# A hybrid mLSTM, attention and expert layer: SBUF pools padded to multiples of 256 bytes

## The chip, the core and the metric

The kernel runs on one core of a Trainium2 chip. The metric is the time that the device needs for one execution, in microseconds (us). The engines have short names in the profile: PE is TensorE (matmuls), PEld its weight loads, DVE is VectorE, ACT is ScalarE, POOL is GpSimd, SP is SyncE, which here only issues transfers. SBUF is the memory that the engines work from: 128 partitions, and a tile has the same byte address in each of its partitions. PSUM is the memory into which PE writes.

## The reference

One encoder layer on 512 tokens of width 2048, in float32, cut here to what matters:

```python
proj = jnp.einsum("bsd,dc->bsc", x, w_in[i])            # 2048 -> 4640 columns
h_mlstm = _mlstm_mixer(mq, mk, mv, mo, mg, ...)         # 8 heads, both directions
h_attn = _axial_gqa(aq, ak, av, g_q[i], g_k[i])         # 8 query heads, 2 key heads of 128
x = _layer_norm(ALPHA * x + concat([h_mlstm, h_attn]) @ w_out[i], ...)
moe = _expert_choice_moe(x, w_router[i], w_gate[i], w_up[i], w_down[i])   # 16 experts, 64 tokens each
pl = sigmoid(x @ w_pl_gate[i] + b_pl_gate[i]) * (p[i] @ w_pl_proj[i])
x = _layer_norm(ALPHA * x + moe + pl, ...)
```

Each expert has three weight matrices of 8 MB (2048 x 1024 gate and up, 1024 x 2048 down); with the gate of pl they are about 400 MB, read once.

## The kernel before, in words

The kernel is written with tiles: a pool is a stretch of SBUF that is opened and closed like a stack, on the left or on the right side, and a tile is a piece of a pool with a name; `bufs` says how many buffers a name has. A scheduler orders the instructions of each engine by their due times and what they depend on, sets the waits, and places a tile in a buffer when the one before it has been read for the last time. Each engine works through its own list in order.

**The projections** (`gemm`, line 178; its matmul is line 197). Each weight block of 512 rows comes into a tile wraw (SP's queue), ACT copies it rounded to fp32r into wH (line 150, `split`) and DVE puts the rest into wL (line 151); the left operand x is split in the same way into xH and xL. Each product is made of three fp32r matmuls: high x high, high x low, low x high. The tiles wraw, wH and wL have two buffers each and take 8 KB of a partition. The attention projection (`attn_proj`, first to run) has four chunks of 392 columns, so a weight tile holds four rows of 392 values, 1568 bytes apart: 4 chunks x 4 blocks x 4 row tiles x 4 rows x 3 are 768 matmuls. The output gate, q and k, v and the two halves of w_out have 512 columns, 1920 matmuls.

**The attention** (`attention`, line 281). Rotary position and norm come group by group (`rope_group`, line 259): ACT squares each head (line 266) into a tile jk that nobody reads, summing into ss; POOL turns the sums into a scale (`pow_rstd`, line 147). First the two key heads (ssk, rk), then the query heads in three groups, (6, 7), (3, 4, 5), (0, 1, 2), each with its own tiles ssq and scq; after each group its heads (`attn_head`, line 314): scores, exp on ACT with scale scq (line 336), the product with v, and a store of oT to DRAM on POOL's queue (line 354). The scheduler lays all this beside the projection of the output gate (`o_proj`, line 356).

**The mLSTM** works from q and k after a convolution (line 478), its gates are turned with the matrix jrev (lines 394, 438, 443), and each head ends with squares into hjk (line 613). Then come w_out in two halves (`mix_attn`, `mix_mlstm`), the layer norm of x1 (`ln1_tile`, with the statistics st and the transposed factors lnT) and the router.

**The experts** (`phase_b`, line 1107) are most of the second half. Weights come as tiles of 1 MB, 8 KB in each of 128 partitions, through a ring of 13 places (`ring_tile`, line 657): four tiles r, opened on the right side for it, the six tiles rw, which are the places of wraw, wH and wL, then l1g, l1b and r3. SP's queue fills them in the order in which they are used: an expert takes 8 gate, 8 up and 8 down tiles (lines 928 and 950) and one of the gate of pl (line 848), and the small tile plp (line 851). PE works through them in a fixed order: gate and up (line 984), pl (line 898) mixed with the sum over the tokens of the expert before (line 1071), down (line 1035). The tokens of an expert are fetched from x1d by an indirect transfer of POOL (line 957).

**Where the tiles lie.** By the memory map of the program, every tile takes a multiple of 32 bytes. The left side begins with small constants; the pool of wraw, wH and wL begins at byte 17824, which is 69 x 256 + 160. All its six tiles lie 160 bytes past a multiple of 256, and so does the first tile of each pool that is set on it. The right side ends at byte 229344, 224 bytes past a multiple of 256: the tiles xH and xL, fa, r, l1g, l1b and r3 all lie at 224. In a weight tile of 392 columns the four rows lie at 160, 192, 224 and 0.

Of the kernel before, what the change touches and what calls it, by code (L numbers as in the profile page):

```python
# [11 lines left out]
F32 = mybir.dt.float32  # L12
# [8 lines left out]
S = 512  # L21
D = 2048
NT = 4
KT = 16
# [69 lines left out]
class Body:  # L94
# [25 lines left out]

    def dump(self, name, t):
        if name in self.dbg:
            self.nc.gpsimd.dma_start(self.dbg[name], t)

    def setup(self):
        nc, a = self.nc, self.a
        c = self.pool("consts")
        self.c = c
        self.ident = c.tile([128, 128], F32, name="ident")
        nc.gpsimd.dma_start(self.ident, a["ident"])  # L130
        self.jrev = c.tile([128, 128], F32, name="jrev")
        nc.gpsimd.dma_start(self.jrev, a["jrev"])
        self.hf = c.tile([128, 1], F32, name="hf")
        nc.gpsimd.dma_start(self.hf, a["half"])
        self.mhalf = c.tile([128, 64], F32, name="mhalf")
        nc.vector.memset(self.mhalf, -0.5)
        d = self.pool("dram", space=DRAM)
        self.ftd = d.tile([D, S], F32, name="ftd")
        self.od = d.tile([S, 1024], F32, name="od")
        self.md = d.tile([16, S], F32, name="md")  # L140
        self.part = d.tile([S, D], F32, name="part")
        self.x1d = d.tile([S, D], F32, name="x1d")
        self.ps = self.pool("psA", space=PSUM)
# [82 lines left out]
    def attn_proj(self):  # L226
        nc = self.nc
        self.mg = self.pool("mgate")
        self.pA = self.pool("projA")
        self.proj = self.pA.tile([128, NT, 1568], F32, name="proj")  # L230
        for ch in (3, 2, 1, 0):
            c0 = ch * 392

            def evac(i, p, c0=c0):
                nc.scalar.copy(self.proj[:, i, c0:c0 + 392], p)

            self.gemm(self.win(3072 + c0, 392), self.xH, self.xL, 392, evac,
                      first=ch == 3)
# [20 lines left out]
    def rope_group(self, nm, c0, n, ss):  # L259
        nc = self.nc  # L260
        ct, st = self.rope[nm]
        for i in range(NT):
            v = self.proj[:, i, c0:c0 + n * 128]
            for h in range(n):
                jk = self.at.tile([128, 128], F32, name="jk", bufs=2)
                nc.scalar.activation(jk, v[:, h * 128:(h + 1) * 128], AF.Square,
                                     accum_out=ss[:, i, h:h + 1])
            v3 = v.rearrange("p (n d) -> p n d", n=n)
            t1 = self.at.tile([128, n, 128], F32, name="t1", bufs=1)
            t2 = self.at.tile([128, n, 128], F32, name="t2", bufs=1)  # L270
            nc.vector.tensor_mul(t1, v3, ct[:, i][:, None, :].to_broadcast([128, n, 128]))
            v5 = v.rearrange("p (n a h f) -> p n a h f", n=n, a=2, h=2)
            t5 = t2.rearrange("p n (a h f) -> p n a h f", a=2, h=2)
            s4 = st[:, i].rearrange("p (a h f) -> p a h f", a=2, h=2)
            for h in range(2):
                nc.vector.tensor_mul(t5[:, :, :, h], v5[:, :, :, 1 - h],
                                     s4[:, :, h][:, None].to_broadcast([128, n, 2, 32]))
            nc.vector.tensor_add(v3, t1, t2)

    def attention(self):  # L280
        nc = self.nc
        self.attn_tables()
        self.at = self.pool("attn")
        at = self.at
        ssk = at.tile([128, NT, 2], F32, name="ssk")
        rk = at.tile([128, NT, 2], F32, name="rk")
        self.rope_group("g_k", GK, 2, ssk)
# [14 lines left out]
        for h0, n in ((6, 2), (3, 3), (0, 3)):  # L302
            ssq = at.tile([128, NT, n], F32, name=f"ssq{h0}")
            scq = at.tile([128, NT, n], F32, name=f"scq{h0}")
            self.rope_group("g_q", GQ + h0 * 128, n, ssq)
            nc.vector.tensor_scalar_add(ssq, ssq, 128 * EPS)
            self.pow_rstd(scq.rearrange("p a b -> p (a b)"), ssq.rearrange("p a b -> p (a b)"))
            for h in range(h0, h0 + n):
                self.attn_head(h, scq, h - h0, kH, kL, vH, vL)

    def attn_head(self, h, scq, hi, kH, kL, vH, vL):
        nc, at = self.nc, self.at
# [8 lines left out]
        for half in range(2):  # L321
            PTH = at.tile([128, NT, 256], F32R, name="PTH", bufs=2)
            PTL = at.tile([128, NT, 256], F32R, name="PTL", bufs=2)
            for q in range(2):
# [5 lines left out]
                nc.tensor.matmul(sp, qL[:, sl], kH[:, kv], start=False, stop=True)  # L330
                sm = at.tile([128, 4], F32, name="sm", bufs=4)
                nc.vector.reduce_max(sm[:, 0:1], sp, axis=AX.X)
# [44 lines left out]
    def gates(self):  # L377
        nc, a = self.nc, self.a
# [3 lines left out]
        g = self.pool("gwork", side="right")  # L382
        G = []
        for nm, b in (("i", "b_i"), ("f", "b_f")):
            t = self.G[nm]
            bt = g.tile([64, 1], F32, name="b" + nm)
            nc.vector.memset(bt, 0.0)
# [67 lines left out]
    def qk_proj(self):  # L455
        nc = self.nc
# [3 lines left out]
        self.QL = self.mq.tile([128, NH, S], F32R, name="QL")  # L460
        cw = self.mq.tile([128, 8, 5], F32, name="cw")
        nc.gpsimd.dma_start(cw, self.a["convT"])
        cv = self.pool("conv")
        lo, hi = slice(0, 64), slice(64, 128)
        for ch in range(2):
            def evac(i, p, ch=ch):
# [3 lines left out]

                r = cv.tile([128, S + 4], F32, name="cr", bufs=2)
                nc.gpsimd.memset(r[:, 0:2], 0.0)
# [108 lines left out]
    def mlstm_num(self, h, ml, hh, P, off, half):  # L581
        nc = self.nc
        pn = [self.ps.tile([128, 512], F32, name=nm, bufs=1) for nm in ("t", "o")]
        for dr in range(2):
            for q in range(2):
                tb = half * 2 + q
                sbs = list(range(0, tb + 1) if dr == 0 else range(tb, NT))
                for k, sb in enumerate(sbs):
                    b = off[dr][sb] + (tb - sb if dr == 0 else tb)
                    nc.tensor.matmul(pn[dr][:, q * 130:(q + 1) * 130],  # L590
                                     P[dr][:, b * 128:(b + 1) * 128], self.v1[:, sb, h],
                                     start=k == 0, stop=k == len(sbs) - 1)
        r = ml.tile([128, 2, 2], F32, name="hr", bufs=4)
        for dr in range(2):
# [12 lines left out]
    def mlstm_post(self, h, ml, hh, o):  # L607
        nc = self.nc
        ss = ml.tile([128, NT], F32, name="hss", bufs=2)
        rs = ml.tile([128, NT], F32, name="hrs", bufs=2)  # L610
        for tb in range(NT):
            jk = ml.tile([128, 128], F32, name="hjk", bufs=1)
# [9 lines left out]
        f = ml.tile([128, S], F32, name="mw", bufs=MW)  # L622
# [47 lines left out]
    def mix_mlstm(self):  # L670
        nc, a = self.nc, self.a
        accp = self.pool("acc")
        self.acc = accp.tile([128, NT, D], F32, name="acc")
        self.st = accp.tile([128, NT, 4, 6], F32, name="bst")
        self.x1T = accp.tile([128, KT, S], F32, name="x1T")
# [3 lines left out]
        nc.gpsimd.dma_start(self.wr[:, :, :NE], a["w_router"])  # L679
        self.lnT = accp.tile([128, 2, KT], F32, name="lnT")  # L680
        nc.gpsimd.dma_start(self.lnT, a["ln1T"])
        self.af = accp.tile([48, 256], F32, name="af")
# [3 lines left out]
        self.bpl = accp.tile([128, KT], F32, name="bpl")  # L686
        nc.gpsimd.dma_start(self.bpl, a["b_plT"])
        fm = self.pool("fm")
        self.close("pa", "fa", "mls2")
        self.r1 = self.pool("r1", side="right")  # L690
        lp = self.r2 = self.pool("r2", side="right")
        g = lp.tile([128, D], F32, name="l1g")
# [412 lines left out]
    def phase_b(self):  # L1105
# [5 lines left out]
        self.sq2 = wk.tile([128, NT, len(LASTW)], F32, name="sq2")  # L1111
        self.m0 = wk.tile([128, NT], F32, name="m0")
        self.r3 = self.pool("r3", side="right")
# [134 lines left out]
```

## Time and profile before

| | us |
|---|---|
| median of 3 runs | 1850.37 |
| lowest and highest of the 3 | 1849.45 and 1853.31 |
| the profiled execution, its own time | 1849.9 |
| its span, from the first to the last instruction | 1847.7 |

| engine | busy us, share of the span | instructions |
|---|---|---|
| PE | 1767.0 (96%) | 8208 |
| PEld | 1039.4 (56%) | 8208 |
| DVE | 755.7 (41%) | 1358 |
| ACT | 408.4 (22%) | 810 |
| POOL | 194.2 (11%) | 255 |

A matmul is counted as busy from its start to a modelled end, and matmuls overlap, so the pace of a row of matmuls is read from the distance of their starts. An fp32 matmul runs as two passes, an fp32r matmul as one, and the profile counts passes. DMA share is the mean busy share of the core's 16 transfer engines; sums of packets that just touch can give 1.01. [...]

### The profile page before, as it was taken

How to read it: one execution, taken by the hardware profiler on the slowest of the kernel's cores; microseconds unless marked ns; L12 is line 12 of the kernel's file. 1: busy time of each engine (PE TensorE's matmuls, PEld its weight loads, DVE VectorE, ACT ScalarE, POOL GpSimd, SP SyncE). 2: the span in 40 equal slices, each digit the busy share in tenths (PEclk: the TensorE clock that was granted, in tenths of full speed). 3: DMA queues.
4: the chain of work that ended last, by engine and by line, in shares of the span. 5: the costliest groups of instructions: out<-in, count | busy, mean ns of one | idle time of the engine just before them, and what ended most of it. 6: DMA issues, size and time to landing. Idle time of an engine off the chain costs nothing.

```text
span 1847.7 us, 20774 instructions
## 1 busy us (share of the span) xinstructions
PE 1767.0 (96%) x8208; PEld 1039.4 (56%) x8208; DVE 755.7 (41%) x1358; ACT 408.4 (22%) x810; POOL 194.2 (11%) x255
## 2 busy tenths in 40 slices
PE   8999999999999999899999999999999999999991
PEld 7998888877777887543443444344334434433441
DVE  4446563593466445711331333133223213322346
ACT  3435453343565212200000000000000000000013
POOL 2000101251133100510000000000000000000004
PEclk9999999999999999989999999999999999999996
DMA  6332223223554782589999999999999999999992
GB/s 219 111 95 95 80 84 94 81 92 98 167 166 133 233 347 92 212 332 409 420 420 420 420 420 420 419 420 420 419 420 420 419 420 421 420 420 419 420 376 91
DMA packets 114066, 535.03 MB, mean 290 GB/s; under 512 B 10641, under 2 KB 26050, under 8 KB 61490
## 3 DMA queue, kind: packets, MB, share of 16 engines
q1 hardware_dynamic: 106082, 504.14, 69.0%
q0 software_dynamic: 7024, 24.07, 3.5%
q10 hardware_dynamic: 864, 5.51, 0.7%
q8 instruction: 64, 1.05, 0.2%
q14 instruction: 32, 0.26, 0.0%
HBM read 514.77 MB, written 18.91 MB: 289 GB/s over the span
## 4 chain that ended last, share of the span: by engine, by line
PE 71%; DMA 19%; DVE 4%; POOL 2%; issue 2%; ACT 2%; SPq 0%; POOLq 0%; ACTq 0%; DVEq 0%
PE g L197 29%; PE pl L898 11%; DMA plp<-in_w_pp_dram 10%; PE py L1035 8%; PE pg L984 5%; DMA r<-in_w_up_dram 5%; PE pu L984 4%; PE pc L1071 3%; DMA rw<-in_w_up_dram 3%; PE plq L892 2%; PE o L350 1%; DMA l1g<-in_w_up_dram 1%; DMA l1b<-in_w_up_dram 1%; PE t L342 1%; ACT mw L540 1%
## 5 line engine op out<-in xcount | busy, mean ns | idle before, releaser
L1073 DVE TENSOR_TENSOR acc<-acc,pc 128x512 f32<-128x512 f32 x240 | 164.6, 687 | 123.9 <-PE pc L1071 122.2
L197 PE MATMUL g<-wH,xH 128*128 128x392 f32 (+1 forms) x512 | 191.2, 375 | 8.9 <-ACT wH L150 8.9
L197 PE MATMUL g<-wH,xL 128*128 128x392 f32 (+1 forms) x512 | 190.4, 372 | 0.0
L151 DVE TENSOR_TENSOR wL<-wraw,wH 128x1024 fp32r<-128x1024 f32 (+2 forms) x114 | 126.4, 1144 | 156.5 <-ACT wH L150 156.5
L197 PE MATMUL g<-wL,xH 128*128 128x392 f32 (+1 forms) x512 | 190.3, 372 | 0.1
L1071 PE MATMUL pc<-ys,oh 128*128 128x512 f32 x240 | 185.6, 774 | 1.1 <-DVE acc L1073 0.9
L150 ACT CAST wH<-wraw 128x1024 fp32r<-128x1024 f32 (+2 forms) x114 | 106.6, 976 | 217.3 <-PE g L197 206.0
L1056 DVE SCALAR_TENSOR_TENSOR ys<-py,gate,ys 64x512 fp32r<-64x512 f32 (+2 forms) x70 | 49.3, 704 | 195.8 <-ACT ys L1052 194.6
L898 PE MATMUL pl<-x1T,rw 128*128 128x512 f32 x224 | 112.3, 592 | 0.0
L197 PEld LDWEIGHTS g<-wH,xH 128*128 128x128 f32 x512 | 97.0, 190 | 19.8 <-ACT wH L150 9.9
L984 PE MATMUL pg<-rw,xeT 128*64 128x512 f32 x480 | 106.0, 593 | 0.0
L957 POOL DMA_INDIRECT xe<-x1d,idx x16 | 15.3, 954 | 857.1 <-PE pc L970 856.7
L1035 PE MATMUL py<-rw,hT 128*64 128x512 f32 x472 | 104.2, 594 | 0.0
L197 PEld LDWEIGHTS g<-wL,xH 128*128 128x128 f32 x512 | 97.1, 190 | 11.1 <-DVE wL L151 1.1
L197 PEld LDWEIGHTS g<-wH,xL 128*128 128x128 f32 x512 | 97.1, 190 | 10.4 <-issue 0.2
L1052 ACT ACTIVATE ys<-py,gate 64x512 fp32r<-64x512 f32 (+2 forms) x70 | 45.2, 646 | 247.2 <-PE py L1035 189.3
L898 PE MATMUL pl<-x1T,r 128*128 128x512 f32 x192 | 98.0, 592 | 0.0
L984 PE MATMUL pu<-rw,xeT 128*64 128x512 f32 x432 | 96.2, 593 | 0.9 <-DMA rw<-in_w_up_dram 0.9
L984 PE MATMUL pg<-r,xeT 128*64 128x512 f32 x416 | 93.3, 600 | 0.0
L990 DVE TENSOR_TENSOR hs<-hs,pu 128x512 f32<-128x512 f32 x16 | 11.0, 688 | 201.2 <-PE pu L984 201.2
L984 PE MATMUL pu<-r,xeT 128*64 128x512 f32 x416 | 92.3, 593 | 1.0 <-DMA r<-in_w_up_dram 1.0
L989 DVE TENSOR_TENSOR hs<-hs,pg 128x512 f32<-128x512 f32 x16 | 11.0, 688 | 176.3 <-ACT hs L988 176.3
(350 smaller groups left out, 2706.8 us busy)
## 6 DMA issues: line engine op xcount, KB each, us to landing
rw<-in_w_gate_dram SPq DMA_DIRECT2D x60, 1024.0 KB, 14.2
rw<-in_w_down_dram SPq DMA_DIRECT2D x59, 1024.0 KB, 17.7
rw<-in_w_up_dram SPq DMA_DIRECT2D x54, 1024.0 KB, 17.9
r<-in_w_gate_dram SPq DMA_DIRECT2D x52, 1024.0 KB, 19.5
r<-in_w_up_dram SPq DMA_DIRECT2D x51, 1024.0 KB, 17.4
r<-in_w_down_dram SPq DMA_DIRECT2D x41, 1024.0 KB, 17.7
wraw<-in_w_in_dram SPq DMA_DIRECT2D x24, 1024.0 KB, 5.0
wraw<-in_w_out_dram SPq DMA_DIRECT2D x16, 1024.0 KB, 7.0
```

The costliest lines, as they stand in the source:

```text
L150: self.nc.scalar.copy(H, src)
L151: self.nc.vector.tensor_sub(L, src, H.bitcast(F32))
L197: self.lastM = nc.tensor.matmul(ps[i][:, :m], l, r, start=beg and q == 0, stop=end and q == 2)
L342: nc.tensor.transpose(pt[:, kb * 128:(kb + 1) * 128], P[:, kb * 128:(kb + 1) * 128], self.ident)
L892: self.pe(nc.tensor.matmul(pp, wp[:, k], self.pT[:, k], start=k == 0, stop=k == 1))
L898: self.pe(nc.tensor.matmul(pg, W[:, k], self.x1T[:, k], start=k == 0, stop=k == KT - 1))
L984: self.pe(nc.tensor.matmul(p[f * 64:(f + 1) * 64], x, lst[g][:, j * 1024 + f * 512:j * 1024 + (f + 1) * 512], start=g == 0 and j == 0, sto ...
L1035: self.pe(nc.tensor.matmul(py[c][n * 64:(n + 1) * 64], hT[:, q // 4, q % 4], Dn[q][:, n * 1024 + c * 512:n * 1024 + (c + 1) * 512], start= ...
L1052: self.lastW = nc.scalar.activation(ys[n][own], py[own], AF.Copy, scale=self.gate[own, e:e + 1])
L1056: nc.vector.scalar_tensor_tensor(ys[n][oth], py[own], self.gate[own, e:e + 1], ys[n][own].bitcast(F32), op0=ALU.mult, op1=ALU.subtract)
L1071: self.pe(nc.tensor.matmul(pc, oh[:, i * 128:(i + 1) * 128], y, start=True, stop=True))
L1073: nc.vector.tensor_add(d, d, pc)
```

## The change

The change alters where tiles lie. A tile of 24 values and one of 56 values are put in as padding, on the left side and on the right; small tiles are made wider (`small` takes a wider tile and hands out its first n columns), the tile cr gets 64 spare columns instead of 4, and a last padding tile closes the first part of the pool acc. After it the ring, the weight tiles, x's halves, the pools' first tiles and nearly all the rest lie on multiples of 256 bytes; the rows of a weight tile of 392 columns lie at 0, 32, 64 and 96. To make room, jk has one buffer instead of two, and the three pairs ssq and scq, which had a name for each group, become two buffers of one name. jrev moves from the constants into the pool mgate (its load is then written after load_x), and the statistics st and lnT to the end of acc's first part. The function `dump`, which nothing calls, goes.

```diff
--- before.py
+++ after.py
@@ -118,9 +118,9 @@
         for n in reversed(list(self.open)):
             self.close(n)
 
-    def dump(self, name, t):
-        if name in self.dbg:
-            self.nc.gpsimd.dma_start(self.dbg[name], t)
+    def small(self, pool, n, name, bufs=1, parts=128, width=64):
+
+        return pool.tile([parts, width], F32, name=name, bufs=bufs)[:, :n]
 
     def setup(self):
         nc, a = self.nc, self.a
@@ -128,12 +128,12 @@
         self.c = c
         self.ident = c.tile([128, 128], F32, name="ident")
         nc.gpsimd.dma_start(self.ident, a["ident"])
-        self.jrev = c.tile([128, 128], F32, name="jrev")
-        nc.gpsimd.dma_start(self.jrev, a["jrev"])
         self.hf = c.tile([128, 1], F32, name="hf")
         nc.gpsimd.dma_start(self.hf, a["half"])
         self.mhalf = c.tile([128, 64], F32, name="mhalf")
         nc.vector.memset(self.mhalf, -0.5)
+        c.tile([128, 24], F32, name="padl")
+        self.pool("padr", side="right").tile([128, 56], F32, name="padr")
         d = self.pool("dram", space=DRAM)
         self.ftd = d.tile([D, S], F32, name="ftd")
         self.od = d.tile([S, 1024], F32, name="od")
@@ -226,6 +226,8 @@
     def attn_proj(self):
         nc = self.nc
         self.mg = self.pool("mgate")
+        self.jrev = self.mg.tile([128, 128], F32, name="jrev")
+        nc.gpsimd.dma_start(self.jrev, self.a["jrev"])
         self.pA = self.pool("projA")
         self.proj = self.pA.tile([128, NT, 1568], F32, name="proj")
         for ch in (3, 2, 1, 0):
@@ -262,7 +264,7 @@
         for i in range(NT):
             v = self.proj[:, i, c0:c0 + n * 128]
             for h in range(n):
-                jk = self.at.tile([128, 128], F32, name="jk", bufs=2)
+                jk = self.at.tile([128, 128], F32, name="jk", bufs=1)
                 nc.scalar.activation(jk, v[:, h * 128:(h + 1) * 128], AF.Square,
                                      accum_out=ss[:, i, h:h + 1])
             v3 = v.rearrange("p (n d) -> p n d", n=n)
@@ -282,8 +284,7 @@
         self.attn_tables()
         self.at = self.pool("attn")
         at = self.at
-        ssk = at.tile([128, NT, 2], F32, name="ssk")
-        rk = at.tile([128, NT, 2], F32, name="rk")
+        ssk, rk = [self.small(at, NT * 2, q, width=32).rearrange("p (a b) -> p a b", a=NT) for q in ("ssk", "rk")]
         self.rope_group("g_k", GK, 2, ssk)
         nc.vector.tensor_scalar(ssk, ssk, 1.0 / 128, EPS, op0=ALU.mult, op1=ALU.add)
         self.pow_rstd(rk.rearrange("p a b -> p (a b)"), ssk.rearrange("p a b -> p (a b)"))
@@ -300,8 +301,8 @@
                 nc.tensor.transpose(pt[:, i * 128:(i + 1) * 128], kv, self.ident)
             self.split(kH[:, h], kL[:, h], pt)
         for h0, n in ((6, 2), (3, 3), (0, 3)):
-            ssq = at.tile([128, NT, n], F32, name=f"ssq{h0}")
-            scq = at.tile([128, NT, n], F32, name=f"scq{h0}")
+            ssq, scq = [self.small(at, NT * n, q, bufs=2, width=32).rearrange("p (a b) -> p a b", a=NT)
+                        for q in ("ssq", "scq")]
             self.rope_group("g_q", GQ + h0 * 128, n, ssq)
             nc.vector.tensor_scalar_add(ssq, ssq, 128 * EPS)
             self.pow_rstd(scq.rearrange("p a b -> p (a b)"), ssq.rearrange("p a b -> p (a b)"))
@@ -328,7 +329,7 @@
                 nc.tensor.matmul(sp, qH[:, sl], kH[:, kv], start=True, stop=False)
                 nc.tensor.matmul(sp, qH[:, sl], kL[:, kv], start=False, stop=False)
                 nc.tensor.matmul(sp, qL[:, sl], kH[:, kv], start=False, stop=True)
-                sm = at.tile([128, 4], F32, name="sm", bufs=4)
+                sm = self.small(at, 4, "sm", bufs=4, width=16)
                 nc.vector.reduce_max(sm[:, 0:1], sp, axis=AX.X)
                 nc.vector.scalar_tensor_tensor(sm[:, 1:2], sm[:, 0:1], -1.0, scq[:, i, hi:hi + 1],
                                                op0=ALU.mult, op1=ALU.mult)
@@ -383,7 +384,7 @@
         G = []
         for nm, b in (("i", "b_i"), ("f", "b_f")):
             t = self.G[nm]
-            bt = g.tile([64, 1], F32, name="b" + nm)
+            bt = self.small(g, 1, "b" + nm, parts=64)
             nc.vector.memset(bt, 0.0)
             for dr in range(2):
                 nc.gpsimd.dma_start(bt[dr * 32:dr * 32 + 8], a[b][dr * 8:dr * 8 + 8])
@@ -458,7 +459,7 @@
         self.KS = self.mq.tile([128, NH, S], F32R, name="KS")
         self.QH = self.mq.tile([128, NH, S], F32R, name="QH")
         self.QL = self.mq.tile([128, NH, S], F32R, name="QL")
-        cw = self.mq.tile([128, 8, 5], F32, name="cw")
+        cw = self.small(self.mq, 40, "cw").rearrange("p (a b) -> p a b", a=8)
         nc.gpsimd.dma_start(cw, self.a["convT"])
         cv = self.pool("conv")
         lo, hi = slice(0, 64), slice(64, 128)
@@ -468,7 +469,7 @@
                 def sub(o, y, h):
                     nc.gpsimd.tensor_sub(o, y, h.bitcast(F32))
 
-                r = cv.tile([128, S + 4], F32, name="cr", bufs=2)
+                r = cv.tile([128, S + 64], F32, name="cr", bufs=2)[:, :S + 4]
                 nc.gpsimd.memset(r[:, 0:2], 0.0)
                 nc.gpsimd.memset(r[:, S + 2:S + 4], 0.0)
                 nc.scalar.copy(r[:, 2:S + 2], p)
@@ -590,7 +591,7 @@
                     nc.tensor.matmul(pn[dr][:, q * 130:(q + 1) * 130],
                                      P[dr][:, b * 128:(b + 1) * 128], self.v1[:, sb, h],
                                      start=k == 0, stop=k == len(sbs) - 1)
-        r = ml.tile([128, 2, 2], F32, name="hr", bufs=4)
+        r = self.small(ml, 4, "hr", bufs=4).rearrange("p (a b) -> p a b", a=2)
         for dr in range(2):
             dn = pn[dr][:, :260].rearrange("p (q c) -> p q c", q=2)[:, :, 128]
             em = (self.aef, self.aeb)[dr][:, half * 2:half * 2 + 2, 1, h]
@@ -606,8 +607,8 @@
 
     def mlstm_post(self, h, ml, hh, o):
         nc = self.nc
-        ss = ml.tile([128, NT], F32, name="hss", bufs=2)
-        rs = ml.tile([128, NT], F32, name="hrs", bufs=2)
+        ss = self.small(ml, NT, "hss", bufs=2)
+        rs = self.small(ml, NT, "hrs", bufs=2)
         for tb in range(NT):
             jk = ml.tile([128, 128], F32, name="hjk", bufs=1)
             nc.scalar.activation(jk, hh[:, tb], AF.Square, accum_out=ss[:, tb:tb + 1])
@@ -671,20 +672,21 @@
         nc, a = self.nc, self.a
         accp = self.pool("acc")
         self.acc = accp.tile([128, NT, D], F32, name="acc")
-        self.st = accp.tile([128, NT, 4, 6], F32, name="bst")
         self.x1T = accp.tile([128, KT, S], F32, name="x1T")
         self.rt = accp
         self.wr = accp.tile([128, KT, 32], F32, name="wr")
         nc.vector.memset(self.wr[:, :, NE:], 0.0)
         nc.gpsimd.dma_start(self.wr[:, :, :NE], a["w_router"])
-        self.lnT = accp.tile([128, 2, KT], F32, name="lnT")
-        nc.gpsimd.dma_start(self.lnT, a["ln1T"])
         self.af = accp.tile([48, 256], F32, name="af")
         nc.vector.memset(self.af, 0.0)
         self.pT = accp.tile([128, 2, S], F32, name="pT")
         nc.gpsimd.dma_start(self.pT, a["pT"].rearrange("(k p) t -> p k t", p=128))
         self.bpl = accp.tile([128, KT], F32, name="bpl")
         nc.gpsimd.dma_start(self.bpl, a["b_plT"])
+        self.st = accp.tile([128, NT, 4, 6], F32, name="bst")
+        self.lnT = accp.tile([128, 2, KT], F32, name="lnT")
+        nc.gpsimd.dma_start(self.lnT, a["ln1T"])
+        accp.tile([128, 48], F32, name="pada")
         fm = self.pool("fm")
         self.close("pa", "fa", "mls2")
         self.r1 = self.pool("r1", side="right")
@@ -1109,7 +1111,7 @@
         nc.scalar.dma_start(self.iota, a["iota"])
         self.sum2 = wk.tile([128, NT, len(LASTW)], F32, name="sum2")
         self.sq2 = wk.tile([128, NT, len(LASTW)], F32, name="sq2")
-        self.m0 = wk.tile([128, NT], F32, name="m0")
+        self.m0 = self.small(wk, NT, "m0", width=16)
         self.r3 = self.pool("r3", side="right")
         xe = self.expert_fetch(0)
         self.pl_early(self.pl_load(0, early=True))
```

## Rows read from the trace of the kernel before

**Rows 1.** The page, section 2: the span in 40 equal slices

```profile
DMA  6332223223554782589999999999999999999992
GB/s 219 111 95 95 80 84 94 81 92 98 167 166 133 233 347 92 212 332 409 420 420 420 420 420 420 419 420 420 419 420 420 419 420 421 420 420 419 420 376 91
```

**Rows 2.** Busy time by stretch: all saturated experts, the late ten, one early expert

```profile
core 0: us, PE busy (x) PEld busy (x) DVE busy (x) ACT busy (x) POOL busy (x), PEclk, DMA share, GB/s
...
1073.25:1715.67 642.42, 630.22 (x2602) 249.89 (x2601) 189.26 (x281) 46.11 (x70) 9.36 (x10) 1.00 1.01 420
825.72:1715.67 889.95, 877.75 (x3625) 347.31 (x3625) 253.55 (x376) 64.56 (x98) 13.12 (x14) 1.00 1.01 419
1010.45:1073.25 62.80, 62.80 (x261) 25.09 (x261) 18.86 (x28) 4.61 (x7) 0.94 (x1) 1.00 1.01 420
```

**Rows 3.** The chain that ended last: start us, us, what

```profile
13.64 137.58 PE g L197 x758
...
597.57 127.39 PE g L197 x546
...
832.36 4.29 PE pl L898 x10
...
1102.74 16.56 DMA rw<-in_w_up_dram
```

**Rows 4.** Busy time by stretch: three stretches of projections (columns as in rows 2)

```profile
46.00:138.00 92.00, 92.00 (x516) 92.00 (x515) 41.63 (x84) 33.47 (x91) 6.20 (x3) 1.00 0.33 103
138.00:297.00 159.00, 159.00 (x860) 130.02 (x860) 95.35 (x206) 79.66 (x170) 12.95 (x20) 1.00 0.26 85
...
598.00:690.00 92.00, 92.00 (x396) 74.13 (x395) 39.47 (x50) 21.22 (x25) 10.64 (x18) 1.00 0.84 295
```

**Rows 5.** Instructions on the tiles jrev and lnT: ns min/median/max, first and last start

```profile
L394 PE MATMUL s<-jrev,Gi x8: 272/273/297, 350.1 to 350.9; 128*32 128x128 f32 x8
...
L132 POOL DMA_DIRECT2D jrev<-in_jrev_dram x1: 574/574/574, 2.1 to 2.1; - x1
...
L756 ACT ACTIVATE x1T<-s,lnT x20: 448/457/484, 734.3 to 767.2; 128x128 f32<-128x128 f32 x20
...
L681 POOL DMA_DIRECT2D lnT<-in_ln1T_dram x1: 540/540/540, 604.2 to 604.2; - x1
```

**Rows 6.** Instructions on the tiles jk and hjk (columns as in rows 5)

```profile
L266 ACT ACTIVATE jk<-proj x40: 293/295/321, 76.6 to 154.6; 128x128 f32<-128x128 f32 x40
...
L613 ACT ACTIVATE hjk<-hh x32: 300/310/328, 506.5 to 593.4; 128x128 f32<-128x128 f32 x32
```

**Rows 7.** Instructions on scq, oT's stores, and the first convolution (columns as in rows 5)

```profile
L336 ACT ACTIVATE P<-s,sm,scq x32: 764/779/787, 161.7 to 295.5; 128x512 f32<-128x512 f32 x32
...
L147 POOL TENSOR_TENSOR scq<-ssq,mhalf x3: 1815/2555/2592, 90.6 to 156.5; 128x12 f32<-128x12 f32 x2, 128x8 f32<-128x8 f32 x1
...
L354 POOL DMA_DIRECT2D ftd<-oT x16: 539/539/626, 170.4 to 305.5; - x16
...
L478 DVE SCALAR_TENSOR_TENSOR cy<-cr,cw,cy x32: 739/751/1871, 343.2 to 415.5; 128x512 f32<-128x512 f32 x32
```

**Rows 8.** DMA queue q1 while rw lands, 914.5:929 and 1549:1563: packets, MB, share

```profile
q1 hardware_dynamic: 833, 6.10, 101.2%
...
q1 hardware_dynamic: 811, 5.88, 101.1%
```

**Rows 9.** DMA queue q1 while l1g, l1b, r3, r land, 1230.5:1247 and 1329.5:1347

```profile
q1 hardware_dynamic: 950, 6.91, 101.0%
...
q1 hardware_dynamic: 1006, 7.33, 101.2%
```

**Rows 10.** PE in order of time: rows at 224 (92.03), 0 (92.56), then 160

```profile
92.03 0.34 PE L197 MATMUL g<-wH,xH 128*128 128x392 f32 x1
...
92.56 0.34 PE L197 MATMUL g<-wH,xH 128*128 128x392 f32 x1
...
93.10 0.34 PE L197 MATMUL g<-wH,xH 128*128 128x392 f32 x1
```

## The prediction

> **What bounds the kernel now.** I read the page's slices first [rows 1]: the transfer engines idle for two thirds of the first 600 us and stand at 9 tenths, 419 to 421 GB/s, from slice 20 to the last but one. Then the windows of that stretch, the sixteen experts [rows 2]: from 825.72 to 1715.67 us, 889.95 us, the DMA share is 1.01 and the rate 419 GB/s, whether the PE waits or not. Until 1073.25 an expert lasts 62.80 us and the PE is busy for all of it: the ring of weight tiles, filled earlier, is being used up. After that ten experts take 642.42 us where ten times 62.80 would be 628.0, so **14.4 us** are spent waiting for weights, and the chain shows for whom: rw<-in_w_up_dram, 16.56 us in one piece [rows 3]. Before the experts it is the other way round: the PE is busy for the whole of the three long stretches of projections [rows 4] and the chain there is L197, 181.5 ns a matmul of 392 columns (137.58 / 758) and 233.3 ns one of 512 (127.39 / 546) [rows 3]. [...] So two things can gain here: the pace of an 8 KB row of a weight tile, up to 14.4 us, and the pace of an L197 matmul, all the way.
>
> **The change part by part.** No instruction goes or comes; what moves are addresses and a few places in queues.
>
> *Queues.* The load of jrev goes behind that of hf on POOL's queue, one issue of 0.57 us; the first reader of jrev comes at 350.1, so 348 us cover it. lnT is issued after pT and bpl instead of before, two issues of 0.54 us later than 604.2; its first reader comes at 734.3 [rows 5]. Nothing on SP's queue moves. Cost: 0.
>
> *One buffer less for jk.* The 40 squares that write jk all run on ACT, which works in order. The same code in the mLSTM part writes hjk with one buffer, and its 32 squares take 310 ns against jk's 295 [rows 6]. 40 x 15 ns is 0.6 us on ACT, in a stretch where the PE has all of 92.00 us of work [rows 4]. Cost: 0, at most 0.6.
>
> *Three pairs ssq, scq become two buffers.* This adds a wait: the third group takes the first group's scq, which heads 6 and 7 read until their last exp. The third scq is now made on POOL at 156.5, ahead of the first exp at 161.7; the 32 exps go on to 295.5, four a head, 16.7 us a head, so head 7 is done near 195 and the group's own first reader, head 0, starts near 245 [rows 7]. It slips by some 40 us and keeps 50 us less 2.6 us of its own. Behind it on POOL stand the stores of oT, which it would hold up only if it were queued ahead of those of heads 6 and 7. If that cover is gone, the attention ends later than 297, and the next reader of its room, the first convolution at 343.2 [rows 7], leaves 46 us. The PE meanwhile has the gate projection: 159.00 of 159.00 us busy [rows 4]. Cost: 0.
>
> *Widened small tiles, cr, bst moved:* the shapes that the engines see are the same. Cost: 0.
>
> *The weight ring.* Before, every ring tile begins off a multiple of 256: the six rw 160 bytes past one, r, l1g, l1b and r3 224 bytes past one. After, all at 0. No DMA of an 8 KB row at 0 is in the trace, so I bound it. Lower end: nothing, or a little worse. Upper end: the whole 14.4 us, since below that the PE is the bound. What lies nearest is the ring itself, the same queue and the same rows at two offsets. Engine time per MB (share x window x 16 / MB): rw 101.2% of 14.5 us for 6.10 MB is 38.49 us, and 38.51 in a later cycle [rows 8]; r and its neighbours 38.59 and 38.66 [rows 9]. Means 38.50 and 38.62: 64 bytes further from the boundary cost 0.3%, or 0.23% by the nearer pair, which is what I take. Carried on in a straight line to 0, rw gains 2.5 steps and r 3.5, on average 3 x 0.23% = 0.7%, and 0.7% of the 889.95 saturated us is **6.2 us**; all of it counts, since the DMA share is 1.01 from the beginning of that stretch. It is an extrapolation, so both ends stay in the range.
>
> *PE operands.* The only moving rows on a multiple of 256 before are the fourth rows of the 392-column weight tiles (160 + 3 x 1568 = 4864 = 19 x 256). Three matmuls from the row at 224 take 0.53 us, three from the row at 0 0.54 us [rows 10]. That gives no gain; it may be 3.3 ns each worse. The weights loaded beside them were at 224 in both, so both operands at 0 is not shown. I take 0 and keep a loss of 3.3 ns and a gain for the rivals. [...]
>
> **Sum.** The profiled execution took 1849.9 us, 1847.7 of span and 2.2 around it; the median of the three runs is 1850.37, 0.5 above. 1849.9 - 6.2 = 1843.7, on the median's scale **1844.2 us**.
>
> **The rivals.**
>
> *The whole wait goes.* If the rows of a weight tile get 1.64% or more faster (14.4 of 875.5 us), the ring never runs dry, all experts last 62.80 us and the time is 1850.4 - 14.4 = 1836.0. For it: the DMA share of 1.01, so any saving in a row is saved in the stretch. Against it: the two offsets of the ring differ by only 0.23 to 0.3% [rows 8, 9]. [...]
>
> *Nothing changes.* The pace of a row is set by something other than its address: 1850.4. For it: the small difference between rw and r, which also lie at opposite ends of the memory. Against it: that the difference has the right sign.
>
> *Slower: aligned operands cost the PE.* Place: every L197 matmul of 512 columns, 1920 of them by the loops. Price: the 3.3 ns of the row at 0, 1920 x 3.3 = 6.4 us, to 1856.8 with no gain in the ring. It decides from 1.9 ns a matmul on if nothing else moves (3.7 us), or from 5.2 ns if the ring gains 6.2. For it: the row at 0 is no faster and by rounding slower. Against it: 10 ns in 530 is the resolution of the view.
>
> [...]
>
> **How the numbers follow.** Forecast 0.31 (3 to 10 us, of it 0.06 below 3.7 us), whole wait gone 0.13, nothing changes 0.30, slower 0.17, PE faster 0.09. A measurement of this kernel can tell 0.2%, 3.7 us, from no change. Faster: 0.25 + 0.13 + 0.09 = 0.47; same 0.36; slower 0.17. The range leaves out the fast PE (0.09) and the far part of the slower case: from 1834, just under the case without waits, to 1857. The forecast's own range is 1840 to 1847.
>
> **What would show it.** Right: in the window of the ten late experts 422 to 423 GB/s instead of 420, experts of some 63.7 us, the chain still with rw<-in_w_up_dram; L197 at 233 and 181 ns; attention's third scq near 200 us and nothing behind it later. Whole wait gone: no DMA piece in the chain of the experts, 62.8 us each. Slower: L197 at 235 ns or more. Wrong in kind: a PE that idles between 138 and 345 us.

## The result, and the profile after

The changed kernel takes 1830.77 us (median of 4 runs, 1829.85 to 1832.22), the kernel before 1851.61 beside it. The ratio is 0.9889, 95% interval 0.9872 to 0.9906: 20.5 us faster, below the low end of the range (1834). The profiled execution has a span of 1827.9 us, 19.8 less than before.

The same slices as [rows 1], of the changed kernel:

```profile
DMA  6322223222554792589999999999999999999982
GB/s 212 121 94 99 78 67 105 93 93 93 161 172 133 225 370 95 197 329 410 426 426 427 426 426 426 426 427 426 426 427 426 426 426 427 426 427 426 427 369 92
```

The transfer engines are as busy as before in the second half, but move 426 GB/s where they moved 420. The windows that answer to [rows 2] (same columns), and the rest of the span:

```profile
820.02:1695.97 875.95, 875.40 (x3626) 349.13 (x3625) 253.23 (x376) 64.54 (x98) 13.13 (x14) 1.00 1.01 425
1067.51:1695.97 628.46, 627.91 (x2600) 251.52 (x2601) 188.94 (x281) 46.10 (x70) 9.37 (x10) 1.00 1.01 426
1004.72:1067.51 62.79, 62.79 (x262) 25.16 (x261) 18.85 (x28) 4.61 (x7) 0.94 (x1) 1.00 1.01 426
1695.97:1827.90 131.93, 93.39 (x480) 44.13 (x480) 67.94 (x127) 26.48 (x61) 22.69 (x10) 0.86 0.69 291
```

The ten late experts take 628.46 us instead of 642.42, and the PE is busy for all but 0.55 us of it; an early expert lasts what it did, 62.79. So the 19.8 us are made of two gains: the saturated stretch is 14.0 us shorter (889.95 to 875.95), and it begins 5.7 us earlier (825.72 to 820.02). The chain that ended last (start us, us, what) shows both:

```profile
33.18 118.17 PE g L197 x663
...
449.06 40.59 PE g L197 x178
...
595.07 123.81 PE g L197 x546
...
1653.41 8.76 PE py L1037 x40
1662.19 15.86 DMA rw<-in_w_up_dram
```

The piece of DMA that stood in the chain of every late expert [rows 3] is left in one of them, at 1662.19. And the long row of w_out (its left operands are fa in the half for the attention and fm in the half for the mLSTM), 546 matmuls, takes 123.81 us where it took 127.39 [rows 3]: 226.8 ns a matmul instead of 233.3. The 392-column row has 178.2 ns (118.17 / 663), but this can't be set against the 181.5 of [rows 3], since that piece begins at 13.64 us and takes in the first matmuls, which are slower: from 14.13 to 17.40 us their starts are 327 ns apart, from 46 to 138 us 178.3 (92.00 / 516). The windows from 46 to 138 us can: 516 matmuls before [rows 4], 519 after, 0.6%.

For the v projection, 178 matmuls of 512 columns that the experiments below are read by, the piece of the kernel before was:

```profile
450.66 41.74 PE g L197 x178
```

That is 234.5 ns, and 228.0 after. Four lines on small things that the prediction spoke of (ns min/median/max, first and last start us):

```profile
L147 POOL TENSOR_TENSOR scq<-ssq,mhalf x3: 1810/2288/2557, 91.2 to 185.4; 128x12 f32<-128x12 f32 x2, 128x8 f32<-128x8 f32 x1
```

```profile
L337 ACT ACTIVATE P<-s,sm,scq x32: 760/778/787, 161.8 to 295.7; 128x512 f32<-128x512 f32 x32
```

```profile
L268 ACT ACTIVATE jk<-proj x40: 309/311/324, 77.2 to 155.0; 128x128 f32<-128x128 f32 x40
```

```profile
L479 DVE SCALAR_TENSOR_TENSOR cy<-cr,cw,cy x32: 735/750/1865, 343.0 to 415.3; 128x512 f32<-128x512 f32 x32
```

The third scq is made at 185.4 instead of 156.5, the squares take 311 ns instead of 295; the exps that read scq still run from 161.8 to 295.7 us, and the first convolution starts at 343.0: no later than before [rows 6, 7].

### The profile page after: what moved, and what is told of

It is laid out like the page before. It is cut to its first block, busy times and chain, and to the rows that moved or that the text cites. A ratio compares the mean times of both kernels' runs of the same rounds, so it can differ in the third digit from the quotient of the medians.

```text
span 1827.9 us, 20774 instructions
## 1 busy us (share of the span) xinstructions
PE 1760.4 (96%) x8208; PEld 1043.9 (57%) x8208; DVE 755.8 (41%) x1358; ACT 411.9 (23%) x810; POOL 195.5 (11%) x255
## 4 chain that ended last, share of the span: by engine, by line
PE 87%; DVE 4%; DMA 4%; POOL 2%; issue 2%; ACT 1%; SPq 0%; POOLq 0%; ACTq 0%; DVEq 0%
PE g L197 28%; PE pg L986 11%; PE pl L900 11%; PE pu L986 11%; PE py L1037 11%; PE pc L1073 3%; PE plq L894 2%; PE o L351 1%; DMA plp<-in_w_pp_dram 1%; DMA wraw<-in_w_in_dram 1%; DMA rw<-in_w_up_dram 1%; PE t L343 1%; PE py L1014 1%; PE t L591 1%; PE o L769 1%
## 5 line engine op out<-in xcount | busy, mean ns | idle before, releaser
L197 PE MATMUL g<-wH,xH 128*128 128x392 f32 (+1 forms) x512 | 190.7, 374 | 8.7 <-ACT wH L150 8.6
L197 PE MATMUL g<-wH,xL 128*128 128x392 f32 (+1 forms) x512 | 189.5, 370 | 0.0
L197 PE MATMUL g<-wL,xH 128*128 128x392 f32 (+1 forms) x512 | 189.3, 370 | 0.1
L197 PEld LDWEIGHTS g<-wH,xH 128*128 128x128 f32 x512 | 97.3, 190 | 18.9 <-ACT wH L150 10.0
L197 PEld LDWEIGHTS g<-wL,xH 128*128 128x128 f32 x512 | 97.4, 190 | 9.9 <-DVE wL L151 1.0
L197 PEld LDWEIGHTS g<-wH,xL 128*128 128x128 f32 x512 | 97.5, 190 | 9.2 <-issue 0.2
## 6 DMA issues: line engine op xcount, KB each, us to landing
r<-in_w_gate_dram SPq DMA_DIRECT2D x52, 1024.0 KB, 19.3
```

What stands on the lines that cost most here:

```text
L197: self.lastM = nc.tensor.matmul(ps[i][:, :m], l, r, start=beg and q == 0, stop=end and q == 2)
```

## The experiments

Most kernels here are the changed one with other sizes of the two first paddings, which move the whole left or right side without changing anything else: padl sets where the weight tiles and the six places rw of the ring lie, and fm with them; padr where the halves of x, fa, r, l1g, l1b and r3 lie. For the left offsets 128 and 32, mhalf is made 32 columns wide instead of 64. Each run is read by two lines: the window from the first plq to the last (columns as in rows 2; plq is the small product that opens an expert's part of pl, so the window holds fourteen experts), and the chain's piece of the v projection.

**The padding alone undone** (left 160, right 224):

```diff
-        c.tile([128, 24], F32, name="padl")
-        self.pool("padr", side="right").tile([128, 56], F32, name="padr")
```

> The changed kernel without its two first padding tiles: the left side lies again 160 and the right side 224 bytes past a multiple of 256, all other edits stay. Theory addresses (the gain comes from where ring and operands lie): all of it goes, 1850 us, experts at 420 GB/s, L197 of 512 columns at 233 ns. Rival others (the narrower jk, the shared ssq and scq, the moved jrev, lnT, bst bring a part): between 1831 and 1850, by what they bring, with 1845 or less to count as a part.

```profile
826.88:1716.35 889.47, 878.01 (x3626) 348.27 (x3625) 253.66 (x376) 64.58 (x98) 13.13 (x14) 1.00 1.01 419
```

```profile
452.78 41.74 PE g L195 x178
...
600.50 125.25 PE g L195 x546
```

1850.11 us, ratio 0.9989 (0.9979 to 0.9999). The experts and the v projection are back where they were, so nearly all of the gain hangs on the two first paddings. The other edits bring at most 0.2%, by the middle of the interval 0.1%, and the row of w_out shows where that can come from: 229.4 ns a matmul, between the 233.3 of before and the 226.8 of after. Its mLSTM half has stayed fast. The matmuls that read fmH, the high part of fm, before and in this run (ns min/median/max; a matmul's time runs to its modelled end):

```profile
L197 PE MATMUL g<-wH,fmH x128: 392/398/796, 647.8 to 756.8; 128*128 128x512 f32 x128
```

```profile
L195 PE MATMUL g<-wH,fmH x128: 389/389/796, 650.7 to 757.1; 128*128 128x512 f32 x128
```

Before, the tiles bst, lnT and bpl stand ahead of fm in the pool acc, 384 + 128 + 64 bytes, so by the tile sizes fm lies 64 bytes off the weights; with bst and lnT moved behind and pada after them it lies at the weights' offset, here 160 for both. So this part too is a matter of addresses.

**Only the left side undone** (left 160, right 0; padl left out) **and only the right side undone** (left 0, right 224; padr left out):

> Only the left side (weight tiles, the six places rw of the ring) goes back to 160, the right side stays at 0. Theory boundary (any start off a multiple of 256 costs an 8 KB row the same): 6 of 13 ring places at 420, 7 at 426, mean 423 GB/s, some 6 to 8 us of waits in the experts. Rival one side (only the right side's tiles gained): 426 GB/s and no wait, or 420 for all if it was the left one. For L197 of 512 columns: 227 ns if the right operand (x, fa, fm) decides, 233 ns if the left one (weights) does, 230 if both do. Time 1837 to 1842 by theory boundary, 1831 or 1850 at the ends.

> The mirror image: the left side at 0, the right side (halves of x, fa, r, l1g, l1b, r3) back at 224. Theory boundary: mean of 7 places at 420 and 6 at 426, 423 GB/s, 7 to 9 us of waits in the experts; rival one side as in the run before, the other way round. L197 of 512 columns: 233 ns if x decides, 227 if the weights do, 230 if both. The gains of this run and of the one before should add to 20.8 us if the two sides act apart.

The first of the two:

```profile
827.43:1705.62 878.19, 875.76 (x3626) 349.25 (x3625) 253.51 (x376) 64.59 (x98) 13.13 (x14) 1.00 1.01 425
```

```profile
453.68 41.91 PE g L196 x178
...
1418.54 15.34 DMA r<-in_w_up_dram
```

The second:

```profile
825.11:1706.13 881.02, 876.53 (x3627) 349.03 (x3625) 253.43 (x376) 64.56 (x98) 13.12 (x14) 1.00 1.01 423
```

```profile
452.83 41.74 PE g L196 x178
...
1353.71 16.63 DMA r<-in_w_up_dram
```

1838.89 us (0.9929, 0.9912 to 0.9946) and 1841.99 us (0.9949, 0.9933 to 0.9966). Neither side is enough for L197: with one operand at 0 and the other not, it is as slow in v as with both off, 41.91 and 41.74 us for 178. So it is not either operand's own place that counts. The ring is in between, as expected, but the waits are smaller than half: 2.2 and 5.1 us more than the 875.95 of the changed kernel, where all places off cost 13.5. A wait comes only when the stock in the ring is used up: the first DMA piece in the chain stands at 1102.74 us before [rows 3], at 1418.54 and 1353.71 here, at 1662.19 after. But the stock is used up before the end in all of them, so it isn't what keeps the waits small. That is the rate, 425 and 423 GB/s, where a mean by places has 422 to 423. The two gains by the ratios, 13.1 and 9.4 us, add to some 22.5, within the noise the 20.5 of the whole.

**Everything at 128, and everything at 32** (padl 24 with the narrow mhalf and padr 24; no padl and padr 48):

> Everything 128 bytes past a multiple of 256, on both sides. Theory boundary 256: the ring is as slow as before, 420 GB/s, waits of 14 us in the experts. Rival 64 bytes (160 and 224 are odd multiples of 32; a multiple of 64 or 128 is as good as 256): 426 GB/s and no wait. Rival count (the price grows with the bytes past the boundary, 1.6% at 160 to 224): about 1.0%, 422 GB/s, 9 us of waits. L197: 227 ns if only 32 odd costs, 233 if 256 is needed.

> Everything 32 bytes past a multiple of 256. Theory boundary: as slow in the experts as at 128, 160 or 224: 419 to 420 GB/s, 13 to 15 us of waits, time 1842 to 1846. Rival count (price by the bytes past the boundary): a quarter or less of it, 424 to 425 GB/s, 1832 to 1836. For L197 of 512 columns: theory equal places (both operands at the same offset from a multiple of 256, whatever it is, as at 0 and at 128) 227 ns; rival multiples of 128 or 64: 233 ns.

At 128:

```profile
822.00:1710.97 888.97, 877.25 (x3626) 348.55 (x3625) 253.63 (x376) 64.57 (x98) 13.13 (x14) 1.00 1.01 420
```

```profile
449.13 40.59 PE g L197 x178
```

At 32:

```profile
823.09:1715.15 892.06, 878.66 (x3626) 347.79 (x3625) 253.65 (x376) 64.54 (x98) 13.13 (x14) 1.00 1.01 418
```

```profile
449.71 40.59 PE g L196 x178
```

1843.69 us (0.9952, 0.9935 to 0.9968) and 1847.06 us (0.9967, 0.9955 to 0.9980). Two answers at once. The ring is slow at both, and at 32 no faster than at 128 (the intervals of the two ratios overlap, so the 3 us between them are not shown): by these rates, 418 and 420 GB/s where the changed kernel has 425 over the same stretch, what counts is to start on the boundary, and the distance from it has no say in the way that the rival count had it. L197 is fast at both, to the hundredth of a microsecond what it is at 0: by these three runs it is enough that its two operands have the same offset, which need not be 0.

**The right side at 128, the left at 0** (padr 24):

> The left side at 0, the right side at 128, so weights and x are 128 bytes apart. L197 of 512 columns: if only equal places are fast, 232 to 234 ns as with 32, 64 and 96 bytes between the two; if a distance of 128 counts as equal, 227 ns. The ring: theory boundary has it as with the right side at 224, 423 GB/s and 9 us of waits; the time is then 1842 with slow L197, 1838 with fast.

```profile
826.20:1704.49 878.29, 876.15 (x3626) 349.02 (x3625) 253.51 (x376) 64.53 (x98) 13.13 (x14) 1.00 1.01 425
```

```profile
451.18 41.73 PE g L197 x178
```

1838.86 us (0.9927, 0.9911 to 0.9944). 128 bytes between the operands are as slow as 32, 64 or 96. The experts wait less than was expected, 2.3 us more than in the changed kernel, though as many places are off as with the right side at 224, where it was 5.1.

**The ring alone at 0** (the halves of x at 224, what comes after them on the right side at 0):

```diff
-        self.pool("padr", side="right").tile([128, 56], F32, name="padr")
...
         self.close("xT3", "xT2", "xT1", "xT0")
+        self.pool("padr", side="right").tile([128, 56], F32, name="padr")
```

> The right side lies at 224 until the halves of x are closed, and at 0 from then on; the left side lies at 0 throughout. So the ring is as in the changed kernel, and only the 512-column projections from x (output gate, q and k, v) have their two operands at different places. Theory two gains (DMA rows in the experts, L197 before them): experts without waits, 62.8 us each, at 426 GB/s; L197 at 233 to 234 ns for x, 227 for w_out; the first expert 2 to 5 us later than in the changed kernel, time 1833 to 1836. Rival (the ring alone makes the difference, the rest is noise of the start): 1831.

```profile
827.10:1703.99 876.89, 875.69 (x3627) 349.12 (x3625) 253.66 (x376) 64.55 (x98) 13.13 (x14) 1.00 1.01 425
```

```profile
305.80 43.40 PE g L196 x186
...
452.81 41.75 PE g L196 x178
...
600.82 119.71 PE g L196 x528
```

1837.18 us (0.9919, 0.9902 to 0.9935), 6.4 us above the changed kernel's median. The experts are within 1 us of those of the changed kernel, the projections from x those of before. The ratio makes this kernel 15.0 us faster than the one before (0.0081 of 1852.03; 12.0 to 18.1 by the interval). Not all of that is the ring: both halves of w_out have their operands alike here too, and run at 226.7 ns a matmul (119.71 / 528). By the windows the experts have 13.1 of it (889.95 to 876.89). What it lacks to the whole, 5.5 us by the ratios, goes with the operands of the projections from x. The time is 1 us above what was expected.

**The two sides of the ring in turn** (as the run with the right side at 224, from the second cycle on in another order of places):

```diff
         k = i % (NR1 + 9)
+        if i >= NR1 + 9:
+            k = (0, 4, 1, 5, 2, 6, 3, 7, 10, 8, 11, 9, 12)[k]
```

> As the run with the right side at 224, but from its second cycle the ring takes places of the two sides in turn, so that a tile of rows at 224 is followed by one of rows at 0. Theory build-up (in the runs with one side off, an 8 KB row at 224 takes the 309 ns of an aligned one at first and 311 to 320 only after some 5 to 10 us of such rows on end, so the engines drift apart and get into each other's way): rows back near 309 to 310 ns, 425 to 426 GB/s, little wait, 1833 to 1836. Rival own price (each row off the boundary costs its own ns, whatever stands before it): 423 GB/s and 1842 as in that run.

```profile
826.88:1707.96 881.08, 876.99 (x3627) 348.87 (x3625) 253.18 (x376) 64.55 (x98) 13.13 (x14) 1.00 1.01 424
```

1842.49 us (0.9948, 0.9931 to 0.9964), and 881.08 us for the experts beside 881.02. The forecast of the theory build-up fails: mixing the tiles saves nothing. But its rival, a price of each row's own, is not shown by that. By that price 6 or 7 of 13 places off would cost about half of the 13.5 us; the runs have 2.2 (six at 160), 2.3 (seven at 128) and 5.1 (seven at 224). In the packets of the same windows an 8 KB row takes 309.8 ns on average in the changed kernel and 315.1 with the padding undone, but 310.4, 310.2 and 311.4 in these three, and 311.2 here. So a row off the boundary costs less while a part of the ring is on it, and why is open.

**The low halves at 32, the high ones at 0**, to see which two operands must lie alike. The padding (shown for w; the pools of x, fa and fm have the same), and P with two buffers:

```diff
         H = w.tile([128, 4, n], F32R, name="wH", bufs=2)
+        if not self.xpad:
+            w.tile([128, 8], F32, name="padw")
         L = w.tile([128, 4, n], F32R, name="wL", bufs=2)
```

The second kernel has the products in another order besides (shown for the case with x on the left; the other case likewise):

```diff
-                    prs = [(xh[:, sl], H[:, j]), (xh[:, sl], L[:, j]), (xl[:, sl], H[:, j])]
+                    prs = [(xh[:, sl], H[:, j]), (xl[:, sl], H[:, j]), (xh[:, sl], L[:, j])]
```

> As the changed kernel, but the low halves (wL, xL, faL, fmL) lie 32 bytes past a multiple of 256 and the high halves at 0; the tile P has two buffers instead of three, for room. In the order high x high, high x low, low x high, the left operand that PE loads for the next matmul is then at the same offset as the right operand that is running, each time; the left operand of the same matmul is so in one of three. Theory next load (the pace suffers when the running right operand and the left operand loaded meanwhile lie at different offsets): 227 ns for L197 of 512 columns. Rival own pair (the two operands of one matmul must lie alike): (227 + 234 + 234) / 3 = 232 ns. Of the ring two places of 13, those of wL, are off: own price in proportion has 425 GB/s, and some 1 to 2 us of waits.

> The same places as in the run before, but the three products in another order: high x high, then the two that were second and third exchanged. Theory next load: two of three matmuls now run while a left operand at another offset is loaded, (227 + 234 + 234) / 3 = 232 ns for L197 of 512 columns, 5 ns more than in the run before from the order alone. Rival own pair: the pairs are the same, so no difference between the two runs, 232 ns in both.

The first:

```profile
452.12 41.55 PE g L202 x178
```

The second:

```profile
456.79 41.55 PE g L202 x178
```

1840.80 us (0.9934, 0.9918 to 0.9951) and 1841.37 us (0.9938, 0.9922 to 0.9955). 233.4 ns a matmul in both, so the theory next load falls: its own case is as slow as the one without. The rival own pair, with one pair of three alike, has 228.0 + 2 x 234.5 by three, 232.3; the mean fits it within 1.1 ns. The single matmuls don't fit it. From one start to the next in the v projection, on average, high x high, high x low and low x high take 233.2, 231.6 and 232.0 ns in the first kernel, and 231.3, 235.7 and 229.5 in the second; in neither does one take 227 and the others 234, and the order of the products has a say. So these runs show that alike in every pair is fast and a mixture is not, and leave open what in the mixture costs. The ring has two of its places off in both, those of wL, and the experts take 877.44 and 875.69 us, at most 1.5 more than in the changed kernel.

**Rows of 4 KB** (the gate, up and down tiles in two transfers each, at 0 and with the paddings left out):

```diff
-                    nc.sync.dma_start(t, w)
+                    for q in (slice(0, 1024), slice(1024, 2048)):
+                        nc.sync.dma_start(t[:, q], w[:, q])
```

> The changed kernel (all at 0) with the experts' gate, up and down tiles loaded in two transfers of half a tile each, so that the rows are of 4 KB instead of 8. The base for the run after this one. A row has some cost of its own, so the rate is lower than 426 GB/s: 414 if a row costs 8 ns beside its bytes, which gives 64.6 us an expert and 20 us more of waits, about 1850.

> The same half rows with the two first paddings left out, so that the left side lies at 160 and the right at 224. Theory per row (a row that starts off the boundary costs 5 ns more, whatever its length): twice as much per MB as with 8 KB rows, the rate 3.0% below the run before (402 if that has 414), some 25 us more. Rival per byte or per time (the engines lose a share of their rate when rows lie off the boundary): 1.5% below (408 if that has 414), some 13 us more.

The slices of the first (all at 0):

```profile
GB/s 214 116 95 96 80 82 94 83 92 99 187 163 124 232 342 91 214 363 404 420 419 420 419 420 419 419 419 419 420 420 415 419 419 420 419 417 419 419 381 91
```

Of the second (left 160, right 224):

```profile
GB/s 213 112 99 89 79 85 102 68 91 110 191 156 127 238 331 75 240 376 407 409 410 410 410 408 410 409 409 409 409 410 407 410 409 409 409 405 409 409 393 90
```

1846.07 us (0.9974, 0.9964 to 0.9984) and 1874.57 us (1.0131, 1.0114 to 1.0148). The rate falls from 419.5 to 409.5 GB/s (middles of the slices), 2.4%, about midway between the two theories, 3.0 and 1.5%. With 16 engines, a row of 8 KB takes 16 x 8192 B / 426 = 307.7 ns at 0 and 312.1 at 420 GB/s, 4.4 more; one of 4 KB takes 156.2 and 160.0 ns, 3.8 more. The packets' own times have 309.8 and 315.1 ns for 8 KB, 5.3 more, and 159.6 and 163.4 for 4 KB, 3.9 more. A price by the row alone would be the same for both, one by the byte half as much for the short row; this lies between, and the run decides for neither. What it shows is that off the boundary short rows lose more: 28.5 us between the two kernels, where rows of 8 KB have 19.3 (1850.11 to 1830.77). L197 has its part in both, and the granted clock in the experts (PEclk, as a share of full speed) is 0.99 in the slower of the two kernels with short rows, 1.00 in the other. At 0 itself two half rows take 312.4 ns for 307.7, 4.7 for the additional row and not the 8 that were supposed.

## Why the prediction was wrong

**Right: where to look.** It named the two paces on which a gain could hang, the row of a ring tile and the matmul of L197, and the bound of the first, 14.4 us. The queues, jk, ssq and scq cost what was written, nothing that a run can tell. (The stretch that it calls the sixteen experts holds fourteen, four and ten; no sum hangs on it.)

**The weight ring: the term was mis-sized by a wrong shape.** The step "carried on in a straight line to 0" took 0.23% for 64 bytes and made 0.7% and 6.2 us of it. The runs show a step: 418 GB/s at 32, 420 at 128, 419 at 160 and 224, 426 at 0. No slope between two points off the boundary can tell of a step on it; the difference of [rows 8, 9] was a small matter beside it. The 1.4% by these rates (425 to 419 over the whole stretch, 426 to 420 in the late ten) is a little under the 1.64% from which the rival "the whole wait goes" was to decide, and this rival is what happened, all but one last wait: 14.0 of 14.4 us, with 0.55 us of idle PE left. It stood with a chance of 0.13.

In these runs the price doesn't grow from 32 bytes to 128: 418 GB/s against 420. With every place off the boundary it is some 4 to 5 ns a row of 8 KB, by rates (312.1 for 307.7) and by packets (315.1 for 309.8).

**PE operands: the step that took 0.** It compared the row at 224 with the row at 0 and noted that the left operands were at 224 in both. That was the very point: 224 with 224 is a pair at the same offset, and the row at 0 was the mismatch. The 10 ns between them [rows 10] are more than rounding: from 46 to 138 us three matmuls take 534.2 ns on average from the rows at 224 and 543.3 from those at 0. But from the rows at 160, 64 bytes off x, they take 530.9, and from 192 538.3. So in the rows of 392 columns a like offset doesn't decide the pace, and they could tell nothing of the rows of 512. The 512-column matmuls, 160 against 224, were all mismatched, and gain 6.5 ns each (233.3 to 226.8). A faster PE has a chance of 0.09 in the forecast, outside the range, and that sign was right. But no run shows the pace that it would need; what the runs showed is 6.5 ns a matmul and 5.7 us, which no case of the forecast had. 1920 x 6.5 ns would be 12.5 us; the chain holds 3.6 of it in the row of 546, 1.15 in the v projection and 0.4 in the longest piece of q and k, and the start of the experts moves by 5.7. Beside the attention, where the exps begin and end as before, nothing is gained; that this is where the rest stays is argued, not shown. The 0 that was taken doesn't hold: 32 bytes between the two operands, with the right side at 224, cost 6.5 ns a matmul (41.74 us for 178 in v, 40.59 in the changed kernel).

**The range.** It reached to each rival alone, the fast PE left out. The two gains don't exclude each other, one lies before the experts and one in them, and together they are 19.7 us in the profile; no case added them.

**Left open.** Why a row off the boundary takes longer, and what in a matmul wants the two operands alike, was not shown. Nor why a ring with half of its places off loses less than half, and more at 224 than at 128.

## What to carry to other kernels

Put the destinations of a stream that saturates the transfer engines on multiples of 256 bytes, above all where its rows are short: off them rows of 4 KB lost 2.4% of their rate, rows of 8 KB 1.4%. Let all operands of a row of fp32r matmuls of 512 columns have the same offset from a multiple of 256; 0, 32 and 128 were alike (40.59 us for 178), 160 by the matmuls that read fmH (389 ns at 160 as at 0, 398 before), and one pair of three alike was not enough (233.4 ns a matmul, 228.0 with all three). And where two gains sit in different stages, add them in one case of the forecast, and don't draw a line to a boundary through points that all lie off it.

## What was not expected of the hardware

The pace of fp32r matmuls of 512 columns hangs on whether the operands' addresses have the same offset from a multiple of 256: 40.59 us for 178 with both at 0, at 32 or at 128, 41.73 to 41.91 us with 32, 64, 96 or 128 bytes between them, 2.8 to 3.3% more. Where the sides are changed, the weights on the left and x running (q and k), 64 bytes cost less than 32. The piece of the kernel before (64 bytes between them):

```profile
304.80 42.62 PE g L197 x186
```

Of the changed one (none):

```profile
305.04 42.20 PE g L197 x186
```

And of the ring alone at 0 (32 bytes), further above: 43.40 us.

The rows of 4 KB at 0 are as slow as the rows of 8 KB off the boundary (419 and 419 to 420 GB/s). And a small deficit of the transfers is hidden for long by the stock of 13 tiles: at 423 and 425 GB/s the first wait came 251 and 316 us later than at 420.
